# One step of a streaming encoder: stores on another queue, output matmuls in turn, other buffer counts, a split compare

## The chip, the cores and the metric

The kernel runs on one core of a Trainium2 chip. A core has TensorE (matmuls, in the profile PE, its weight loads PEld), VectorE (DVE), ScalarE (ACT), GpSimd (POOL) and SyncE (SP), which only issues DMAs here. The metric is device microseconds of one execution: the median of the runs.

## The reference

One layer with width 1024 for 1,152 rows: 1,024 of a prompt and 128 of 8 decoding requests with 2,048 cached rows each. Everything is fp32.

```
n1 = rmsnorm(h);  z = n1 @ w_in  -> q_a k_a v_a | forget logits | q_b k_b v_b | gate_a gate_b
A: 8 heads x 64, causal, logit += sum of log f between key and query   (keys and queries normalised)
B: 8 heads x 64, own chunk of 64 and the 8 before it, clipped relative bias
m = sigmoid(gate_a)*(y_a @ w_up_a) + sigmoid(gate_b)*(y_b @ w_up_b);   h += m @ w_out
h += PEER(rmsnorm(h))     # per head: top 16 of 128 keys in each of two halves, top 16 of their sums,
                          # softmax g; sum over 8 x 16 of g*gelu(u[idx].x)*v[idx], 16,384 experts
h += sigmoid(rmsnorm(h) @ w_ple_gate) * (p @ w_ple_proj)
```

The outputs are h for both groups of rows, and the new keys, values and log forget values of both branches.

## The kernel before, in words

Rows go in 9 tiles of 128 (tile 8 holds the decoding rows), in two groups: tiles 8, 0, 1, 2, then tiles 3 to 7. The instructions of each engine run in order, and that order is set when the kernel is built, by a scheduler that takes the operations by priority and by its own model of time; `high_priority(offset=...)` with a negative offset marks filling work.

Stages for the first group: norm, attention (`attention_phase`), merge with gates, routing (top 16 of keys on VectorE). Then the second group through the same stages, while under them the experts of the first group's tiles are fetched row by row: GpSimd issues an indirect DMA (L813) into a ring of 4 buffers, VectorE multiplies and accumulates (L816, L818). There are 1,024 of these gathers; 400 are laid as filling before the second attention, the other 624 are tied to steps of the last loop. The second group's experts are computed densely: 36 of 128 hidden blocks (`hidden_phase`) as filling in the second routing, stored to DRAM (L974); then `expand_phase` builds the routing weights as a sum of products of one-hot rows; then `dense_phase` loops over 128 blocks of 128 experts.

Attention runs over 8 units of two heads, four of branch A and four of branch B. `project` makes for each tile of a unit keys, queries and values (three matmuls per slice, split into high and low parts), normalises them (a power on GpSimd, L217), stores the keys and values to the outputs (L328, L329), transposes them, copies the keys into `kT` (L345) and scales the queries into `qp` (L348). In the first group, keys and values of prompt tiles also go to DRAM for the second group (L350, L351). The scores of a tile follow one unit later (`prompt`, or `decode` for tile 8): for each of the two heads scores, minimum, exponential, scaling, transposes (`pt`, L494) copied to `pT` by ScalarE, and the product with the values into one half of the columns of bank `po` (L497). Both heads share `po`, taken at the start of `prompt`. In branch A a second matmul adds the forget sums, with the stationary operand `sel_p`, a constant selector of 8 x 128 columns made at the start by GpSimd (`setup_masks`, L141 called at L169 and L170) and VectorE (L171).

`decode` loads the cache in tiles of 256 KB into buffers with tag `kc` (L522, L586; `KC` = 15 of them, which the temporaries of `setup_masks` use first). Its four requests per pass go to four groups of 32 columns in turn (L547, L591).

In `expand_phase` each of 80 blocks of 8 entries makes one-hot rows `oa` of the first index (L917) and `ob` of the second (L920) on VectorE, scales the first by the routing weight (`ga`, GpSimd L924 and ScalarE L929 in alternate blocks), multiplies on TensorE (L933) and copies to `stage` (L935), stored per half tile (L939).

The DMAs of loads and stores all go through SyncE's queue, in order, except the indirect ones.

Of the kernel before, what the change touches and what calls it, by code (L numbers as in the profile page):

```python
# [18 lines left out]
P = 128  # L19
# [5 lines left out]
GROUPS = ([8, 0, 1, 2], [3, 4, 5, 6, 7])  # L25
DENSE = (3, 4, 5, 6, 7)
PRE = tuple(range(3, 128, 4)) + tuple(range(1, 128, 32))
KC = 15
NP = 4
SM = 6  # L30
PB = (2, 2)
# [15 lines left out]
def build(tc, I, O, dbg=None, stop=None):  # L47
# [44 lines left out]
    nc.vector.memset(m_corner[64:128, :], BIG)  # L92
    m_new = [const.tile([P, P], BF, name=f"m_new{s}") for s in range(2)]
    m_blk = [const.tile([P, P], BF, name=f"m_blk{s}") for s in range(2)]
    sel_p = const.tile([P, 8, P], F32R, name="sel_p")
    qn = const.tile([P, 2], F32, name="qn")
    kn = const.tile([P, 2, P], F32, name="kn")
    bfv = const.tile([P, 8], F32, name="bfv")
# [31 lines left out]
    def setup_masks(dec):  # L130
# [18 lines left out]
        for s in range(2):  # L149
# [10 lines left out]
            nc.vector.tensor_tensor(c, c, d_, op=OP.min)  # L160
            nc.vector.tensor_tensor(a, a, c, op=OP.max)
            nc.vector.tensor_copy(m_new[s], a)
        for q in range(2):
            t1 = tmp(f"t1{q}").rearrange("p (h c) -> p h c", h=4)
            t2 = tmp(f"t2{q}").rearrange("p (h c) -> p h c", h=4)

            o3 = one.rearrange("p (h c) -> p h c", h=4)
            for t, off in ((t1, 4 * q), (t2, 32 + 4 * q)):
                keep(t, o3, [[-1, 4], [0, P]], 0.0, -off, 1)  # L169
                keep(t, t, [[1, 4], [0, P]], 0.0, off, -1)  # L170
            nc.vector.tensor_tensor(sel_p[:, 4 * q:4 * q + 4, :], t1, t2, op=OP.add)  # L171
        for q in range(2):
            t1 = tmp(f"t1{q}s").rearrange("p (h c) -> p h c", h=4)
            t2 = tmp(f"t2{q}s").rearrange("p (h c) -> p h c", h=4)
# [85 lines left out]
    def attention_phase(g, tiles, aT, yT):  # L260
# [17 lines left out]
        def load_unit(u):  # L278
            br = u // 4
            ws = wload(I["wu"][u], 8, 384, f"wu{g}{u}", extra=I["wfl"] if u == UNITS[0] else None,  # L280
                       eng=nc.vector if (u == UNITS[0]) == (g == 0) else None) if g == 0 else wload(I["wu"][u], 8, 384, f"wu{g}{u}", extra=I["wfl"] if u == UNITS[0] else None, eng=nc.gpsimd if u in UNITS[0:NP] else None)
            kT = at.tile([P, WK], F32, tag="kT", name=f"kT{g}{u}")
            vU = at.tile([P, npr + (TS in tiles), P], F32, tag="vU", name=f"vU{g}{u}")
            hi = min(x for x in tiles if x != TS)
            if hi > 0:
                lo = 0 if br == 0 else max(0, hi - 4)
                if lo < hi:
                    nc.sync.dma_start(kT[:, lo * P:hi * P], kT_d[u, :, lo * P:hi * P])
                    nc.sync.dma_start(vU[:, lo:hi, :], v_d[u, :, lo:hi, :])
            Dn = None  # L290
            if br == 1:
                Dn = at.tile([P, 2, 256], F32, tag="Dn", name=f"Dn{g}{u}")
                nc.sync.dma_start(Dn, I["biasP"][u - 4])
                for h in range(2):
                    hh = 2 * (u - 4) + h
                    nc.vector.tensor_scalar(Dn[:, h, :], Dn[:, h, :], rb0[:, hh:hh + 1], -1.0,
                                            op0=OP.subtract, op1=OP.mult)
                    nc.vector.memset(Dn[0:64, h, 192:256], BIG)
            return ws, kT, vU, Dn

        def project(u, n, t, ws, kT, vU, Dn):
# [23 lines left out]
            else:  # L325
                ko = None
            if ko is not None:
                nc.sync.dma_start(ko[rows, cu * P:(cu + 1) * P], kq[:, 0:P])  # L328
                nc.sync.dma_start(vo[rows, cu * P:(cu + 1) * P], vt)  # L329
            tp = bank(f"tp{nm}")  # L330
            nc.tensor.transpose(tp[:, 0:P], kq[:, 0:P], ident)
            nc.tensor.transpose(tp[:, P:2 * P], kq[:, P:2 * P], ident)
            qp = at.tile([P, 2, P], F32, tag="qp", name=f"qp{nm}", bufs=2 * nts if g == 0 else nts + 1)
            nc.gpsimd.memset(qp, 0.0)
            if t == TS:
                kTs = at.tile([P, P], F32, tag="kTs", name=f"kTs{nm}")
                nc.scalar.copy(kTs, tp[:, 0:P])
                q4 = qp.rearrange("p a c -> p (a c)").rearrange("p (b h i) -> p b h i", b=8, h=2)
                for h in range(2):
                    s = slice(64 * h, 64 * h + 64)  # L340
                    nc.scalar.activation(q4[s, :, h, :], tp[s, P:2 * P].rearrange("p (b i) -> p b i", i=16),
                                         AF.Copy, scale=qn[s, br:br + 1])
                pending.append(decode(u, br, qp, kTs, vU[:, slot[TS], :], n, at, dec, yT))
            else:
                nc.scalar.copy(kT[:, t * P:(t + 1) * P], tp[:, 0:P])  # L345
                for h in range(2):
                    s = slice(64 * h, 64 * h + 64)
                    nc.scalar.activation(qp[s, h, :], tp[s, P:2 * P], AF.Copy, scale=qn[s, br:br + 1])  # L348
                if g < len(GROUPS) - 1:
                    nc.sync.dma_start(kT_d[u, :, t * P:(t + 1) * P], kT[:, t * P:(t + 1) * P])  # L350
                    nc.sync.dma_start(v_d[u, :, t, :], vt)  # L351
                pending.append([lambda: prompt(g, u, br, t, n, qp, kT, vU, Dn, at, yT)])

        def order(p):
# [25 lines left out]
    def logf(g, tiles, fl, at, dec):  # L380
# [29 lines left out]
            nc.tensor.transpose(ps[0:40, 0:P], l40[:, i, :], ident)  # L410
            nc.scalar.copy(lT[:, i, :], ps[0:40, 0:P])
        for i, t in enumerate(tiles):
            nc.sync.dma_start(O["lf"][:, t * P:(t + 1) * P], lT[0:8, i, :])
        pt = [t for t in tiles if t != TS]
        if pt:
            i0 = tiles.index(pt[0])
# [35 lines left out]
    def prompt(g, u, br, t, n, qp, kT, vU, Dn, at, yT):  # L452
# [1 line left out]
        nk = t + 1 if br == 0 else min(t, 4) + 1  # L454
        k0 = t + 1 - nk
        W = nk * P
        po = bank(f"po{nm}")
        both = W <= 512 and wide[0] == 1024
        for h in range(2):
            if h == 0 or not both:  # L460
# [2 lines left out]
            for c0 in range(0, W, 512):  # L463
# [2 lines left out]
                rhs = kT[:, k0 * P + c0:k0 * P + c1]  # L466
                if br == 0:
                    nc.tensor.matmul(N[:, c0:c1], qp[:, h, :], rhs, start=True, stop=False)
                    nc.tensor.matmul(N[:, c0:c1], sel_p[:, 2 * u + h, :], cP[:, c0:c1], start=False, stop=not last)
                    if last:  # L470
                        nc.tensor.matmul(N[:, W - P:W], ident_b, m_diag, start=False, stop=True)
                else:
# [17 lines left out]
            for j0 in range(0, nk, 4):  # L490
# [2 lines left out]
                for j in range(j0, j1):  # L493
                    nc.tensor.transpose(ps[:, (j - j0) * P:(j - j0 + 1) * P], p[:, j * P:(j + 1) * P], ident)  # L494
                evac(pT[:, j0:j1, :], ps[:, 0:(j1 - j0) * P].rearrange("p (j c) -> p j c", c=P))
            for j in range(nk):
                nc.tensor.matmul(po[64 * h:64 * h + 64, 0:P], vU[:, k0 + j, 64 * h:64 * h + 64], pT[:, j, :],  # L497
                                 start=j == 0, stop=j == nk - 1)
        nc.scalar.copy(yT[:, u, n * P:(n + 1) * P], po[:, 0:P])

    def decode(u, br, qp, kTs, vU, n, at, dec, yT):
# [383 lines left out]
    def expand_phase():  # L885
# [22 lines left out]
        for n, t in enumerate(DT):  # L908
            rb, gT = ready
            for c0 in range(0, P, W):  # L910
                if c0 % 64 == 0:
# [2 lines left out]
                oa = ex.tile([P, 2, P, 4], BF, tag="oa", name=f"oa{t}_{c0}")  # L914
                ga = ex.tile([P, W, P], F32, tag="ga", name=f"ga{t}_{c0}")
                ob = ex.tile([P, W, P], F32, tag="obb", name=f"obb{t}_{c0}")
                nc.vector.tensor_tensor(oa, iota_i.unsqueeze(1).broadcast_to([P, 2, P, 4]),  # L917
                                        rb[:, 0, cw].rearrange("p (b c) -> p b c", b=2).unsqueeze(2).broadcast_to([P, 2, P, 4]),
                                        op=OP.is_equal)
                nc.vector.tensor_tensor(ob, iota, rb[:, 1, cw].unsqueeze(2).broadcast_to([P, W, P]), op=OP.is_equal)  # L920
                for b in range(2):
                    if (c0 // W) % GD == 0:
# [13 lines left out]
                if c0 == 64 and n + 1 < len(DT):  # L936
                    ready = prepare(DT[n + 1])
                if c0 % 64 == 64 - W:
                    nc.sync.dma_start(G_d[2 * n + c0 // 64], stage)  # L939
        st.close()  # L940

    nsp = -(-TD // 512)
# [26 lines left out]
    def hidden_phase(dn, n2h, n2l):  # L969
        with tc.high_priority(offset=FILL):  # L970
            for q, j in enumerate(PRE):
                ge = dn.tile([P, TD], F32, tag="ge", name=f"gp{j}")
                hidden(dn, ge, j, n2h, n2l, nc.gpsimd, True)
                nc.sync.dma_start(ge_d[q], ge)  # L974

    def dense_phase(hp, yacc, n2h, n2l):

# [219 lines left out]
```

## Time and profile before

| | |
|---|---|
| median of 3 runs | 4042.02 us (4021.49 to 4048.87) |
| the profiled execution | 4036.04 us, span 4033.9 us |
| granted TensorE clock, mean | 0.966 |
| TensorE busy | 3674.5 us (91% of the span) |
| VectorE busy | 2939.1 us (73%) |
| GpSimd busy | 1865.5 us (46%) |
| ScalarE busy | 1446.2 us (36%) |
| DMA | 1002.50 MB, 249 GB/s over the span |

Busy time of an engine is the union of its instructions; matmuls are pipelined, so a single one lasts longer than its distance to the next. A window row gives busy time and count of instructions for a stretch. In rows of waits, "A <- B: total, times, longest" says that A's engine stood idle until B ended. SPq and POOLq are the queues from which DMAs are issued.

### The profile page before, as it was taken

To read this page: it belongs to the slowest core of one execution; us is meant where nothing else is said; L and a number is where in the kernel's file an instruction comes from. 1 tells how busy PE (TensorE), PEld (TensorE's weight loads), DVE (VectorE), ACT (ScalarE), POOL (GpSimd) and SP (SyncE) were. 2 spreads that over 40 slices of the span, in tenths; PEclk is the share of its full clock that TensorE was granted. 3 is DMA by queue.
4 is the path that set the end of the run, shared out by engine and by line. 5 is a ranking of instruction groups with operands and counts; after the bars stand their busy time and mean duration, and the time that the engine had idled before them with its cause. 6 is when DMAs were issued, how large, how long until landed. Compare 5 with 4: busy or idle time off the path is not lost.

```text
span 4033.9 us, 57386 instructions
## 1 busy us (share of the span) xinstructions
PE 3674.5 (91%) x20520; PEld 3032.9 (75%) x20520; DVE 2939.1 (73%) x5531; ACT 1446.2 (36%) x3307; POOL 1865.5 (46%) x1440
## 2 busy tenths in 40 slices
PE   7998899868888798899898899999999999999989
PEld 6555567656676565699898888888888888888866
DVE  5122202899887776889998698888888888888862
ACT  5444422346555510223488422222222222222231
POOL 5111032127667655553276355555555555555510
PEclk9999999879999999899999999999999999999999
DMA  6777733328888888983345789988989898989942
GB/s 207 239 237 208 229 96 120 103 74 262 276 284 263 285 317 297 329 268 115 109 189 219 274 307 310 320 311 310 330 313 317 307 325 314 325 302 307 313 159 72
DMA packets 415118, 1002.50 MB, mean 249 GB/s; under 512 B 38816, under 2 KB 170352, under 8 KB 412400
## 3 DMA queue, kind: packets, MB, share of 16 engines
q0 software_dynamic: 147456, 536.94, 38.7%
q1 hardware_dynamic: 267376, 461.90, 34.4%
q8 instruction: 161, 2.64, 0.3%
q14 instruction: 125, 1.02, 0.1%
HBM read 917.19 MB, written 81.50 MB: 248 GB/s over the span
## 4 chain that ended last, share of the span: by engine, by line
PE 30%; DVE 19%; DMA 19%; issue 18%; POOL 12%; ACT 2%; SPq 0%; POOLq 0%; DVEq 0%; ACTq 0%
DMA v<-in_pv,gi 7%; POOL u L813 6%; DMA u<-in_pu,gi 6%; PE hd L964 5%; POOL v L813 3%; DVE gya L818 3%; DVE u L816 3%; PE pg L933 3%; PE Sd L547 2%; PE py L1015 2%; PE py L1017 2%; PE py L1016 2%; PE pu L638 1%; DMA vs<-in_pv 1%; PE z L209 1%
## 5 line engine op out<-in xcount | busy, mean ns | idle before, releaser
L813 POOL DMA_INDIRECT v<-in_pv,gi x512 | 680.3, 1329 | 582.8 <-DVE gya L818 451.2
L813 POOL DMA_INDIRECT u<-in_pu,gi x512 | 663.4, 1296 | 505.7 <-DVE u L816 374.8
L816 DVE SCALAR_TENSOR_TENSOR u<-u,gn 128x1024 f32<-128x1024 f32 x512 | 628.2, 1236 | 169.0 <-DMA u<-in_pu,gi 167.3
L818 DVE SCALAR_TENSOR_TENSOR gya<-v,hid,gya 128x1024 f32<-128x1024 f32 x512 | 661.3, 1292 | 120.0 <-DMA v<-in_pv,gi 115.5
L1015 PE MATMUL py<-vh,wh 128*128 128x512 f32 x1280 | 507.7, 398 | 44.2 <-ACT wh L946 23.6
L964 PE MATMUL hd<-aTh,uh 128*128 128x320 f32 x2048 | 485.1, 314 | 24.0 <-ACT gp L967 13.7
L1017 PE MATMUL py<-vh,wl 128*128 128x512 f32 x1280 | 498.3, 395 | 5.8 <-DVE wl L947 5.5
L1016 PE MATMUL py<-vl,wh 128*128 128x512 f32 x1280 | 502.8, 394 | 0.0
L964 PE MATMUL hd<-aTh,ul 128*128 128x320 f32 x2048 | 484.1, 314 | 5.5 <-DVE ul L947 4.2
L964 PE MATMUL hd<-aTl,uh 128*128 128x320 f32 x2048 | 484.1, 313 | 0.0
L964 PEld LDWEIGHTS hd<-aTh,uh 128*128 128x128 f32 x2048 | 351.9, 191 | 35.1 <-ACT gp L967 15.0
L964 PEld LDWEIGHTS hd<-aTh,ul 128*128 128x128 f32 x2048 | 349.6, 190 | 12.6 <-DVE ul L947 6.9
L964 PEld LDWEIGHTS hd<-aTl,uh 128*128 128x128 f32 x2048 | 351.3, 191 | 4.0
L1015 PEld LDWEIGHTS py<-vh,wh 128*128 128x128 f32 x1280 | 242.9, 190 | 102.3 <-ACT wh L946 29.7
L946 ACT CAST vh<-vs 128x1024 fp32r<-128x1024 f32 x128 | 134.0, 1052 | 483.3 <-DMA vs<-in_pv 241.9
L1017 PEld LDWEIGHTS py<-vh,wl 128*128 128x128 f32 x1280 | 243.2, 190 | 61.2 <-DVE wl L947 10.6
L1016 PEld LDWEIGHTS py<-vl,wh 128*128 128x128 f32 x1280 | 242.9, 190 | 46.9
L946 ACT CAST uh<-us 128x1024 fp32r<-128x1024 f32 x128 | 134.2, 1048 | 293.0 <-PE hd L964 285.3
L946 ACT CAST wh<-ge 128x640 fp32r<-128x640 f32 x128 | 91.9, 727 | 402.7 <-DVE ge L993 213.4
L1018 DVE TENSOR_TENSOR yacc<-yacc,py 128x1024 f32<-128x1024 f32 x160 | 192.5, 1215 | 15.0 <-PE py L1017 15.0
L497 PE MATMUL po<-pT,vU 128*64 128x128 f32 x1056 | 153.0, 290 | 34.6 <-ACT pT L80 34.0
L933 PE MATMUL pg<-obb,ga 128*128 128x128 f32 x1280 | 158.8, 279 | 26.5 <-POOL ga L924 19.5
(1051 smaller groups left out, 7361.0 us busy)
## 6 DMA issues: line engine op xcount, KB each, us to landing
us<-in_uT SPq DMA_DIRECT2D x128, 512.0 KB
vs<-in_pv SPq DMA_DIRECT2D x128, 512.0 KB
G_d<-stage SPq DMA_DIRECT2D x10, 4096.0 KB
gj<-G_d SPq DMA_DIRECT2D x64, 640.0 KB
kcd<-in_kA SPq DMA_DIRECT2D x128, 256.0 KB
vcd<-in_vA SPq DMA_DIRECT2D x128, 256.0 KB
ge_d<-gp SPq DMA_DIRECT2D x36, 320.0 KB
ge<-ge_d SPq DMA_DIRECT2D x36, 320.0 KB
```

What stands on the lines that cost most here:

```text
L497: nc.tensor.matmul(po[64 * h:64 * h + 64, 0:P], vU[:, k0 + j, 64 * h:64 * h + 64], pT[:, j, :], start=j == 0, stop=j == nk - 1)
L547: nc.tensor.matmul(ps[32 * b4:32 * b4 + 32, :], q3[:, 4 * s + b4, :], rhs, start=br == 1 and q < nch, stop=True)
L813: nc.gpsimd.indirect_dma_start(out=r, out_offset=None, in_=I["pu" if k < P else "pv"], in_offset=bass.IndirectOffsetOnAxis(ap=gi[:, kk:kk ...
L816: nc.vector.scalar_tensor_tensor(r, r, 1.0, n2, op0=OP.mult, op1=OP.mult, accum_out=hid[:, kk:kk + 1])
L818: nc.vector.scalar_tensor_tensor(ya, r, hid[:, kk:kk + 1], ya, op0=OP.mult, op1=OP.add)
L933: nc.tensor.matmul(pg[:, c * P:(c + 1) * P], ga[:, b0 + c, :], ob[:, b0 + c, :], start=True, stop=True)
L946: nc.scalar.copy(out_h, src)
L964: nc.tensor.matmul(ps[sp][:, 0:Nw], a[:, k, :], b[:, k, sp * Nw:(sp + 1) * Nw], start=k == 0 and q == 0, stop=k == 7 and q == 2)
L1015: nc.tensor.matmul(py[:, c], wh[:, ns], vh[:, c], start=a, stop=False)
L1016: nc.tensor.matmul(py[:, c], wh[:, ns], vl[:, c], start=False, stop=False)
L1017: nc.tensor.matmul(py[:, c], wl[:, ns], vh[:, c], start=False, stop=z)
L1018: nc.vector.tensor_tensor(yacc[n], yacc[n], py, op=OP.add)
```

## The change

`KC` goes from 15 to 18. `sel_p` becomes 8 columns wide, built by four selects over 8 columns, and is repeated over 128 columns where it is read. `qp` has 6 buffers in place of 8 in the first group, `Dn` (bias) one in place of two. The stores of keys, values, log forget values, the scratch keys and values, the hidden blocks and the routing weights move from SyncE to ScalarE's queue; that of the keys stands behind the copy to `kT`. In `prompt` the products with the values come after both heads' transposes, the two heads in turn for each block of keys, and `po` is taken there. `oa` is made by two compares of 512 columns in place of one of 1,024.

```diff
-KC = 15
+KC = 18
-    sel_p = const.tile([P, 8, P], F32R, name="sel_p")
+    sel_p = const.tile([P, 8], F32R, name="sel_p")
-        for q in range(2):
-            t1 = tmp(f"t1{q}").rearrange("p (h c) -> p h c", h=4)
-            t2 = tmp(f"t2{q}").rearrange("p (h c) -> p h c", h=4)
-            o3 = one.rearrange("p (h c) -> p h c", h=4)
-            for t, off in ((t1, 4 * q), (t2, 32 + 4 * q)):
-                keep(t, o3, [[-1, 4], [0, P]], 0.0, -off, 1)
-                keep(t, t, [[1, 4], [0, P]], 0.0, off, -1)
-            nc.vector.tensor_tensor(sel_p[:, 4 * q:4 * q + 4, :], t1, t2, op=OP.add)
+        t1 = tmp("t1")[:, 0:8]
+        t2 = tmp("t2")[:, 0:8]
+        for t, off in ((t1, 0), (t2, 32)):
+            keep(t, one[:, 0:8], [[-1, 8]], 0.0, -off, 1)
+            keep(t, t, [[1, 8]], 0.0, off, -1)
+        nc.vector.tensor_tensor(sel_p, t1, t2, op=OP.add)
...
-                Dn = at.tile([P, 2, 256], F32, tag="Dn", name=f"Dn{g}{u}")
+                Dn = at.tile([P, 2, 256], F32, tag="Dn", name=f"Dn{g}{u}", bufs=1)
...
             if ko is not None:
-                nc.sync.dma_start(ko[rows, cu * P:(cu + 1) * P], kq[:, 0:P])
-                nc.sync.dma_start(vo[rows, cu * P:(cu + 1) * P], vt)
+                nc.scalar.dma_start(vo[rows, cu * P:(cu + 1) * P], vt)
...
-            qp = at.tile([P, 2, P], F32, tag="qp", name=f"qp{nm}", bufs=2 * nts if g == 0 else nts + 1)
+            qp = at.tile([P, 2, P], F32, tag="qp", name=f"qp{nm}", bufs=nts + 2 if g == 0 else nts + 1)
...
                 nc.scalar.copy(kT[:, t * P:(t + 1) * P], tp[:, 0:P])
+                if ko is not None:
+                    nc.scalar.dma_start(ko[rows, cu * P:(cu + 1) * P], kq[:, 0:P])
...
-                    nc.sync.dma_start(kT_d[u, :, t * P:(t + 1) * P], kT[:, t * P:(t + 1) * P])
-                    nc.sync.dma_start(v_d[u, :, t, :], vt)
+                    nc.scalar.dma_start(kT_d[u, :, t * P:(t + 1) * P], kT[:, t * P:(t + 1) * P])
+                    nc.scalar.dma_start(v_d[u, :, t, :], vt)
...
-            nc.sync.dma_start(O["lf"][:, t * P:(t + 1) * P], lT[0:8, i, :])
+            nc.scalar.dma_start(O["lf"][:, t * P:(t + 1) * P], lT[0:8, i, :])
...
-        po = bank(f"po{nm}")
+        pTs = []
...
-                    nc.tensor.matmul(N[:, c0:c1], sel_p[:, 2 * u + h, :], cP[:, c0:c1], start=False, stop=not last)
+                    nc.tensor.matmul(N[:, c0:c1], sel_p[:, 2 * u + h:2 * u + h + 1].broadcast_to([P, P]), cP[:, c0:c1], start=False, stop=not last)
...
-            for j in range(nk):
-                nc.tensor.matmul(po[64 * h:64 * h + 64, 0:P], vU[:, k0 + j, 64 * h:64 * h + 64], pT[:, j, :],
-                                 start=j == 0, stop=j == nk - 1)
+            pTs.append(pT)
+        po = bank(f"po{nm}")
+        for j in range(nk):
+            for h, pT in enumerate(pTs):
+                r = slice(64 * h, 64 * h + 64)
+                nc.tensor.matmul(po[r, 0:P], vU[:, k0 + j, r], pT[:, j, :], start=j == 0, stop=j == nk - 1)
...
-                nc.vector.tensor_tensor(oa, iota_i.unsqueeze(1).broadcast_to([P, 2, P, 4]),
-                                        rb[:, 0, cw].rearrange("p (b c) -> p b c", b=2).unsqueeze(2).broadcast_to([P, 2, P, 4]),
-                                        op=OP.is_equal)
+                for b in range(2):
+                    nc.vector.tensor_tensor(oa[:, b, :, :], iota_i,
+                                            rb[:, 0, c0 + 4 * b:c0 + 4 * b + 4].unsqueeze(1).broadcast_to([P, P, 4]), op=OP.is_equal)
...
-                    nc.sync.dma_start(G_d[2 * n + c0 // 64], stage)
+                    nc.scalar.dma_start(G_d[2 * n + c0 // 64], stage)
...
-                nc.sync.dma_start(ge_d[q], ge)
+                nc.scalar.dma_start(ge_d[q], ge)
```

## Rows read from the trace of the kernel before

**Rows 1.** Busy time by stage: stretch, its length, engines with instructions, clock, DMA share, GB/s

```profile
core 0: us, PE busy (x) PEld busy (x) DVE busy (x) ACT busy (x) POOL busy (x), PEclk, DMA share, GB/s
17.00:505.00 488.00, 428.32 (x3379) 285.32 (x3378) 135.74 (x370) 242.33 (x820) 111.46 (x137) 0.96 0.75 223
700.00:890.00 190.00, 139.78 (x599) 113.78 (x598) 171.66 (x939) 76.28 (x202) 31.48 (x32) 0.85 0.27 86
890.00:1395.00 505.00, 443.41 (x2524) 341.93 (x2522) 425.05 (x820) 301.76 (x850) 354.83 (x301) 0.96 0.83 270
1395.00:1690.00 295.00, 254.37 (x933) 176.87 (x934) 219.97 (x312) 47.70 (x65) 160.39 (x134) 0.94 0.88 310
1690.00:2015.00 325.00, 293.36 (x1824) 282.88 (x1822) 302.75 (x1270) 114.65 (x191) 130.31 (x79) 0.93 0.54 178
2015.00:2165.00 150.00, 146.18 (x1163) 145.39 (x1164) 137.52 (x100) 122.75 (x318) 104.45 (x55) 0.99 0.53 202
2257.00:3860.00 1603.00, 1543.96 (x8193) 1367.66 (x8192) 1370.88 (x1513) 376.56 (x535) 850.01 (x621) 0.99 0.90 314
```

**Rows 2.** Waits of TensorE from 17 to 505 us: total, times, longest

```profile
PE pod L591 <- DMA vcd<-in_vA: 25.6, 22, 2.4
PE z L209 <- ACT vU L318: 13.0, 3, 9.2
```

**Rows 3.** Selects at L141 (ns min/median/max, first to last start), then instructions in time

```profile
L141 POOL TENSOR_SCALAR_AFFINE_SELECT t<-one x4: 635/661/705, 25.9 to 28.1; 128x512 f32<-128x512 f32 x4
L141 POOL TENSOR_SCALAR_AFFINE_SELECT t<-t x4: 631/636/677, 34.3 to 38.5; 128x512 f32<-128x512 f32 x4
...
34.92 1.02 POOL L217 TENSOR_TENSOR kq048r<-kq048r,half 128x4 f32<-128x4 f32 x1
36.76 0.69 PE L209 MATMUL z<-wu04h,aTh 128*128 128x392 f32 x1 [9.20 <-ACT vU L318]
```

**Rows 4.** Output matmuls in time (start, us), then busy time of L497 by stage

```profile
1215.63 1.74 PE L497 MATMUL po<-pT,vU 128*64 128x128 f32 x14 [0.35 <-ACT pT L80]
346.74 3.04 PE L591 MATMUL pod<-vcd,pTd 128*32 128x128 f32 x102 [0.16 <-ACT pTd L80]
...
17.00:505.00 488.00, 33.22 (x192) 21.14 (x192) 0.96 0.75 223
890.00:1395.00 505.00, 118.36 (x859) 95.58 (x857) 0.96 0.83 270
```

**Rows 5.** Gathers (L813) by stretch: GpSimd busy (count); then VectorE's use, 890 to 1395

```profile
890.00:1395.00 505.00, 283.80 (x229) 0.96 0.83 270
1395.00:1690.00 295.00, 156.54 (x130) 0.94 0.88 310
1500.00:1600.00 100.00, 56.94 (x49) 0.98 0.87 301
...
L816 DVE SCALAR_TENSOR_TENSOR u<-u,gn 128x1024 f32<-128x1024 f32 x128 | 161.1, 1264 | 31.2 <-DMA u<-in_pu,gi 30.8
```

**Rows 6.** Waits in SyncE's queue over the span: total, times, longest

```profile
SPq L974 <- ACT gp L967: 172.8, 25, 16.9
SPq L329 <- ACT vU L318: 141.8, 36, 16.9
SPq L328 <- DVE kq L316: 90.3, 31, 12.0
```

**Rows 7.** A key store on SyncE's queue: ns min/median/max, first to last start

```profile
L328 SPq DMA_DIRECT2D out_kA<-kq x36: 332/344/1157, 63.7 to 1276.5; - x36
```

**Rows 8.** A round of the one-hot loop in time; a wait for the compare; a 512-wide row

```profile
2209.32 3.48 POOL L924 TENSOR_TENSOR ga<-oa,gT 128x512 f32<-128x512 bf16 x2 [2.24 <-ACT stage L935]
2212.84 0.69 DVE L917 TENSOR_TENSOR oa<-iota_i,rb 128x1024 bf16<-128x1024 bf16 x1 [0.94 <-POOL ga L924]
2214.99 2.08 POOL L924 TENSOR_TENSOR ga<-oa,gT 128x512 f32<-128x512 bf16 x1 [2.19 <-PE pg L933]
...
POOL ga L924 <- DVE oa L917: 11.5, 7, 6.2
...
L789 DVE TENSOR_TENSOR oh<-oh 128x512 bf16<-128x512 bf16 x20 | 12.4, 622 | 0.1
```

More of the change, by code (lines that the diff above doesn't have):

```diff
@@ L345, in project @@
                 nc.scalar.copy(kT[:, t * P:(t + 1) * P], tp[:, 0:P])
+                if ko is not None:
+                    nc.scalar.dma_start(ko[rows, cu * P:(cu + 1) * P], kq[:, 0:P])
                 for h in range(2):
```

## Prediction

> **What bounds the kernel now.** I first cut the span into its stages, by the lines that run in each, and read the busy time of every engine per stage [rows 1]. The reader is to see there that no engine bounds the whole. The first attention (17 to 505) is TensorE's: 428 of 488 us busy, VectorE 136. Routing of the first group (700 to 890) is VectorE's, 172 of 190. The second attention (890 to 1395) has TensorE at 443 of 505, but VectorE at 425 as well. The second merge (1395 to 1690) is TensorE's again; routing of the second group (1690 to 2015) is VectorE's, 303 of 325; the expert loop (2257 to 3860) holds 1544 of 1603 us on TensorE, and no line of the diff runs in it. So the change can only pay in the two attentions, at the start, and in 1690 to 2257.
>
> Second, who TensorE waited for in the first attention [rows 2]: 25.6 us for cached values still on their way, 13.0 us for ScalarE's copy of a value tile, 9.2 of them in one piece at 27 to 37 us [rows 3]. Third, the two kinds of probability-times-value matmuls in order of time [rows 4]. Fourth, how many gathers start in each stage [rows 5], because 400 of the 1,024 gathers are laid as filling under everything from 890 us on. Fifth, what SyncE's queue stood for [rows 6] and what one store costs it [rows 7]. Last, one round of the one-hot loop [rows 8].
>
> **Start: the selector.** Eight selects over 512 columns go (4 x 0.661 + 4 x 0.636 = 5.2 us of GpSimd [rows 3]); four over 8 columns come. No row has 8 columns; between nothing and the old price each, I take a quarter, as start-up must dominate. This matters because GpSimd's queue holds the power for the first row norms: it runs at 34.92 behind four of those selects and one more (3.3 us), and TensorE's stall ends right after, at 36.76 [rows 3]. Gain: 3.3 x 3/4 = 2.5, say **-3 us** (bounds 0 and -5.2). Its use as a stationary operand with a repeated column changes no count of loads; I cost it at nothing.
>
> **Two heads' outputs in turn.** Today 14 such matmuls in a row, all into the same 64 columns of the array, take 1.74 us, 0.124 each; in decode, where four neighbours go to four different quarters of 32 columns, 102 take 3.04 us, 0.030 each [rows 4]. Four quarters together cost what one half costs alone, so instructions on different columns run at the same time. With two halves in turn I expect 0.124 per pair, 0.062 each (bounds: 0.124, no overlap, and 0.062, both at once). There are 1,056 of them: 192 in the first attention and 864 in the second (859 recorded) [rows 4]. TensorE saves 192 x 0.062 = 12 us there and 864 x 0.062 = 54 us here. In the first attention TensorE is the bound, so **-12 us** (bounds 0, -12). The output bank is also taken later, after both heads' transposes, which frees a bank for these; the price is that both transposed tiles live until the end, with only two buffers. I count these against each other.
>
> **Stores on ScalarE's queue, more cache buffers.** 56 key and 56 value stores, 24 + 24 to the scratch tensors and 9 of gates leave SyncE; 92 of these 169 fall in the first attention, 77 in the second. What SyncE loses on them is not the issue, 0.34 us each [rows 7], but standing: 141.8 us for the value copy and 90.3 for the keys [rows 6], with the next loads queued behind. Without them, and with 18 cache buffers in place of 15 (a score pass loads 16 tiles), loads start earlier; the smaller query and bias buffers that pay for them give back some depth. The stake is the 25.6 us of [rows 2]; I take half, **-13 us** (bounds 0, -25.6). The Trainium skill speaks against this: its page "DMA: Bandwidth & Descriptors", section "Issuing engines are not separate DMA queues", says that all queues end on the same 16 DMA engines and that issuing from several saves only the issuing sequencer's time, usually small. By that rule this term would be nothing. The rows show something the rule leaves out, the in-order wait before the issue, so I keep half.
>
> ScalarE pays. No row shows a store on its queue; SyncE's 0.344 us is the nearest [rows 7]. In the first attention 92 x 0.344 = 32 us come on top of 242 busy of 488 [rows 1]. They stand behind copies that TensorE needs (value tile, key tile), and what follows them, the query scaling, is used one unit later; that is the cover. If it were gone all 32 us would count. I take **+4 us** (bounds 0, +32). Each store waits for data already made: the value or key copy just ahead of it on the same engine, or keys that the transposes have already read. Queued behind it are the query copies and the next softmax.
>
> **The second attention.** TensorE needs 54 us less, but the gathers don't. The stage starts 229 gathers in 505 us, 0.453 per us; the merge after it, where VectorE has far less else to do, 130 in 295, 0.441; the best 100 us have 49 [rows 5]. So the gathers already go at about their own pace, and VectorE works them off in order between the softmax steps. If the order of instructions keeps 229 of them in the stage, it can shrink to 229 / 0.49 = 467 us at best, -38, and not at all at the merge's pace. If they are pushed out instead, 54 x 0.453 = 24 gathers of 1.26 us on VectorE [rows 5] = 31 us land in the routing stage, whose VectorE has 22 us free of 325 [rows 1]: net 54 - 31 = -23. Between 0, -23 and -38 I take **-16 us**. The 77 stores (26 us on ScalarE, 302 of 505 busy) hide behind the gathers' pace; without that cover they are the slower rival below.
>
> **Routing to expansion.** SyncE's 172.8 us of standing for the hidden activations [rows 6] go, but TensorE is busy 293 of 325 and 146 of 150 there [rows 1]. The one-hot compare becomes two of 512. Nearest row: 512 bf16 at 0.622 us [rows 8], so 1.24 against 0.69; lower bound, no cost. In a late round the compare is done at 2213.5 and GpSimd needs it only at 2214.99, after TensorE [rows 8]: 1.46 us of cover. In 2015 to 2165 VectorE has 12.5 us free and ran 100 instructions [rows 1], two a block, so 50 of the 80 blocks: 50 x 0.55 = 27.5, so up to +15; against it, GpSimd's 11.5 us of waiting for this compare could go [rows 8]. I take **0**.
>
> **Sum**: -3 - 12 - 13 + 4 - 16 = **-40 us**. The profiled execution took 4036.04 us (span 4033.9), so 3996; it lies 6 us below the median 4042.02, so on the median's scale 4002. I predict **4000 us**, own range 3980 to 4020.
>
> **Rivals.**
> *All of it arrives*: cached values never late and gathers at their best pace: -3 - 12 - 25.6 + 4 - 38 = -75, 3961 us. For it: 49 gathers in 100 us do occur. Against: no whole stage holds that pace.
> *ScalarE becomes the bound (slower)*: the stores stand in its in-order queue ahead of the softmax of both attentions. All 169 x 0.344 = 58 us on the path and no gain in the second attention: -3 - 12 - 13 + 58 = +30, 4066 us; with a quarter of SyncE's 232 us of standing [rows 6] moved along, 4124. It decides from 44 / 169 = 0.26 us per store on the path, where the gains are used up. Against: ScalarE is busy half and 60% of the two stages.
> *Loads gain nothing* (the shared-engines rule as a mechanism here: transfers, not the queue, are late): 4000 + 13 = 4013 us. The DMA engines are 75% busy in that stage [rows 1], which fits either.
> *The halves don't overlap*: no 12 and no 16: 4028 us. Against: the decode matmuls [rows 4].
> *Nothing moves the end*: 4042 us; the attention would have to be bound by VectorE or loads throughout.
>
> **Chances.** Forecast 0.42, all arrives 0.15, loads gain nothing 0.12, no overlap 0.07, nothing 0.05, ScalarE 0.19. A measurement of this kernel tells about 1%, 40 us, from no change: below 4002 lie all of the second and two thirds of the forecast's cases, 0.43; above 4082 some three quarters of ScalarE's, 0.15; between, 0.42. Range 3945 to 4065: it leaves out the worst of ScalarE's cases and little below.
>
> **What would show it.** Pairs of output matmuls at about 0.06 us each; the first attention ending 20 to 30 us earlier, with waits for cached values about half; the second attention shorter by 10 to 25 us at an unchanged 0.45 to 0.47 gathers per us; the stall at 27 to 37 us shorter by about 3; the expert loop at 1603 us. It is wrong if ScalarE's stores cost well over 0.34 us or TensorE waits for ScalarE much more; if the gathers pile up in the routing stage; or if the new order of instructions changes the expert loop.

## The result, and the profile after

The changed kernel takes 4000.59 us in the median of 10 runs (3988.24 to 4012.65), the kernel before 4037.78 beside it (10 runs, 4021.49 to 4048.87): ratio 0.9917, interval 0.9901 to 0.9932, so 0.8% faster. The predicted time of 4000 is met; by the bound of 1% named there the outcome is "no change". The profiled execution after took 3997.34 us (span 3995.6, mean granted clock 0.962).

To see where 38 us of span went, both traces are cut at the same marks of the program instead of at the same times: the last decode output (end of the first attention), the first gather, the last output matmul (end of the second attention), the last merge matmul, the last top index, the first matmul of the expansion, the expert loop. The columns are those of [rows 1]. First the kernel before, then the changed one:

```profile
17.00:503.00 486.00, 427.41 (x3373) 284.87 (x3375) 135.74 (x370) 240.71 (x817) 111.21 (x136) 0.96 0.75 223
892.70:1391.50 498.80, 440.58 (x2517) 340.80 (x2516) 419.53 (x799) 297.89 (x842) 351.94 (x299) 0.96 0.83 271
1391.50:1685.50 294.00, 253.91 (x930) 176.06 (x929) 218.74 (x309) 47.63 (x64) 159.99 (x134) 0.94 0.88 309
1685.50:2023.80 338.30, 302.20 (x1872) 291.40 (x1871) 313.08 (x1281) 121.51 (x208) 139.04 (x85) 0.93 0.54 181
2279.70:3874.00 1594.30, 1537.05 (x8111) 1358.61 (x8112) 1368.93 (x1510) 370.62 (x527) 849.39 (x621) 0.99 0.90 312
```

```profile
17.00:467.40 450.40, 405.08 (x3377) 279.44 (x3375) 131.47 (x369) 238.92 (x817) 107.49 (x134) 0.96 0.80 240
859.20:1335.70 476.50, 400.80 (x2526) 305.42 (x2525) 406.91 (x796) 295.62 (x846) 330.19 (x286) 0.94 0.82 270
1335.70:1622.30 286.60, 253.53 (x934) 175.45 (x930) 217.78 (x290) 47.99 (x65) 158.92 (x131) 0.93 0.89 313
1622.30:1980.40 358.10, 316.88 (x1973) 305.27 (x1972) 339.60 (x1313) 123.76 (x210) 166.83 (x102) 0.94 0.59 199
2237.10:3834.80 1597.70, 1537.02 (x8111) 1360.30 (x8112) 1368.93 (x1510) 370.93 (x527) 847.50 (x621) 0.99 0.89 311
```

The first attention is 35.6 us shorter with the same matmuls: TensorE is busy 22.3 us less and idle 13.3 us less (58.6 to 45.3). The second attention is 22.3 us shorter, though TensorE's work in it fell by 39.8. The merge gains 7.4. Routing of the second group then gives 19.8 back, the expert loop, in which no line changed, 3.4, and the stretches that the rows leave out 3.8. That 3.4 means little: over the traces with all their gathers laid as before, the loop takes 1584 to 1605 us.

In the first attention, TensorE's costliest groups; before first, and only the two that matter, since the third stands in [rows 4]:

```profile
L547 PE MATMUL Sd<-kcd,qp 128*32 128x512 f32 x320 | 100.5, 615 | 1.8 <-DVE Nd L557 1.2 <-DMA kcd<-in_kA 0.6
L591 PE MATMUL pod<-vcd,pTd 128*32 128x128 f32 x1280 | 52.0, 284 | 26.9 <-DMA vcd<-in_vA 25.6 <-ACT pTd L80 1.1
```

```profile
L550 PE MATMUL Sd<-kcd,qp 128*32 128x512 f32 x320 | 89.7, 603 | 0.7 <-DMA kcd<-in_kA 0.7
L594 PE MATMUL pod<-vcd,pTd 128*32 128x128 f32 x1280 | 43.0, 274 | 5.0 <-DMA vcd<-in_vA 3.1 <-ACT pTd L80 1.8
L501 PE MATMUL po<-pT,vU 128*64 128x128 f32 x192 | 28.3, 325 | 16.7 <-ACT pT L80 16.6
```

The wait for cached values is almost gone (25.6 to 3.1, [rows 2]). What the prediction had not looked at is the busy time: decode's score matmuls (`Sd`) cost 10.8 us less and its output matmuls (`pod`) 9.0 less, with the same counts. The prompt's output matmuls (`po`) give 4.9, and 9 us more are waited for ScalarE's copies in front of them; decode's transposes (`ptd`, L579) take 6.3 back (27.1 to 33.4). How the same `Sd` matmuls can cost different times is seen in the kernel before, in order of time (start, length):

```profile
201.60 1.07 PE L547 MATMUL Sd<-kcd,qp 128*32 128x512 f32 x8
...
211.03 1.06 PE L547 MATMUL Sd<-kcd,qp 128*32 128x512 f32 x6
212.02 0.33 PE L494 MATMUL pt<-ident,p 128*128 128x128 f32 x1
212.27 1.05 PE L547 MATMUL Sd<-kcd,qp 128*32 128x512 f32 x2
```

One matmul of a request leaves two records, so x8 is all four requests, each on its own 32 columns of the array: 1.07 us together. At 211.03 three run (x6) and the fourth follows alone behind another matmul (x2): 1.06 + 1.05, twice the cost. TensorE waits for nothing there. Its order is fixed when the kernel is built, so it is the scheduler that put the other matmul between them; that it did so because its model has the fourth tile come late is an inference, and that the tile was late in the run is not shown. The price is paid as busy time and not as idle time, since a lone quarter costs as much as four. Over the stage the kernel before has 91 such bursts (records of `Sd` that start one after the other), 53 of them with one or two records; the changed one 87 and 46. Bursts of all four are not more but fewer (13 and 9): what goes is short ones.

The other lines that answer to the prediction's are of the changed kernel too, but for one: the output matmuls of one head, six records, of the kernel before.

```profile
104.40 0.87 PE L497 MATMUL po<-pT,vU 128*64 128x128 f32 x6
```

The changed kernel in order of time, the start and some output matmuls of both attentions:

```profile
25.31 0.49 POOL L141 TENSOR_SCALAR_AFFINE_SELECT t<-one 128x8 f32<-128x8 f32 x2
32.28 0.35 POOL L141 TENSOR_SCALAR_AFFINE_SELECT t<-t 128x8 f32<-128x8 f32 x2
33.51 1.02 POOL L215 TENSOR_TENSOR kq048r<-kq048r,half 128x4 f32<-128x4 f32 x1
35.35 0.69 PE L207 MATMUL z<-wu04h,aTh 128*128 128x392 f32 x1 [8.03 <-ACT vU L316]
...
104.54 0.43 PE L501 MATMUL po<-pT,vU 128*64 128x128 f32 x2
105.49 0.87 PE L501 MATMUL po<-pT,vU 128*64 128x128 f32 x10
...
155.95 0.43 PE L501 MATMUL po<-pT,vU 128*64 128x128 f32 x2 [3.69 <-ACT pT L80]
157.34 1.54 PE L501 MATMUL po<-pT,vU 128*64 128x128 f32 x10
...
1202.98 1.09 PE L501 MATMUL po<-pT,vU 128*64 128x128 f32 x14
```

The power runs at 33.51 and the stall ends at 35.35, 1.4 us earlier than in [rows 3]. 14 output matmuls take 1.09 us where they took 1.74 [rows 4]. The ten at 157.34 take 1.54 us where the same ten at 105.49 take 0.87; TensorE has just waited 3.69 us for ScalarE, and the granted clock is 0.50, the lower of its two levels (1.2 GHz):

```profile
157.30:158.70 1.40, 1.40 (x11) 1.14 (x10) 0.00 (x0) 0.58 (x1) 0.00 (x0) 0.50 0.97 256
```

By stretch, TensorE's time on L501 around the second attention, then GpSimd's on the gathers (L816) in the second attention, the merge, and routing up to the last top index:

```profile
850.00:1400.00 550.00, 61.57 (x864) 49.26 (x864) 0.93 0.82 271
...
859.20:1335.70 476.50, 261.18 (x214) 0.94 0.82 270
1335.70:1622.30 286.60, 156.74 (x128) 0.93 0.89 313
1622.30:1847.40 225.10, 79.66 (x63) 0.95 0.76 255
```

L501's 61.57 us stand against 119.81 in the same stretch before; the gathers, 214, 128 and 63, against 227, 131 and 48. TensorE's whole work in the second attention fell by less than L501's, 39.8 against 58.2, for the other matmuls cost more there (the 96 of L468 655 ns in the mean, 628 before) at a granted clock of 0.94 where it was 0.96. Last, a value store on ScalarE's queue (ns min/median/max), the answer to [rows 7]:

```profile
L326 ACTq DMA_DIRECT2D out_vA<-vU x36: 338/339/397, 63.6 to 1225.8; - x36
```

### The profile page after: what moved, and what is told of

The parts are those of the page before. It is cut to its first block, busy times and chain, and to the rows that moved or that the text cites. A ratio compares the mean times of both kernels' runs of the same rounds, so it can differ in the third digit from the quotient of the medians.

```text
span 3995.6 us, 57332 instructions
## 1 busy us (share of the span) xinstructions
PE 3616.7 (91%) x20520; PEld 2993.2 (75%) x20520; DVE 2956.2 (74%) x5610; ACT 1438.8 (36%) x3307; POOL 1848.0 (46%) x1436
## 4 chain that ended last, share of the span: by engine, by line
DVE 23%; issue 21%; DMA 21%; PE 20%; POOL 13%; ACT 2%; POOLq 0%; ACTq 0%; SPq 0%; DVEq 0%
DMA v<-in_pv,gi 9%; POOL u L816 7%; DMA u<-in_pu,gi 6%; POOL v L816 4%; DVE gya L821 4%; DVE u L819 4%; PE pg L936 2%; PE Sd L550 2%; DMA vs<-in_pv 1%; PE pu L641 1%; PE hd L967 1%; POOL ga L927 1%; PE z L207 1%; DVE topi L735 1%; PE z L209 1%
## 5 line engine op out<-in xcount | busy, mean ns | idle before, releaser
L816 POOL DMA_INDIRECT v<-in_pv,gi x512 | 668.6, 1306 | 597.6 <-DVE gya L821 442.5
L816 POOL DMA_INDIRECT u<-in_pu,gi x512 | 673.9, 1316 | 500.5 <-DVE u L819 359.4
L1018 PE MATMUL py<-vh,wh 128*128 128x512 f32 x1280 | 510.3, 400 | 60.8 <-DVE yacc L1021 39.8
L967 PE MATMUL hd<-aTh,uh 128*128 128x320 f32 x2048 | 485.0, 314 | 13.9 <-ACT gp L970 12.2
L936 PEld LDWEIGHTS pg<-obb,ga 128*128 128x128 f32 x1280 | 152.2, 191 | 42.8 <-POOL ga L927 20.7
```

The lines of the kernel that those rows point to most:

```text
L816: nc.gpsimd.indirect_dma_start(out=r, out_offset=None, in_=I["pu" if k < P else "pv"], in_offset=bass.IndirectOffsetOnAxis(ap=gi[:, kk:kk ...
L936: nc.tensor.matmul(pg[:, c * P:(c + 1) * P], ga[:, b0 + c, :], ob[:, b0 + c, :], start=True, stop=True)
L967: nc.tensor.matmul(ps[sp][:, 0:Nw], a[:, k, :], b[:, k, sp * Nw:(sp + 1) * Nw], start=k == 0 and q == 0, stop=k == 7 and q == 2)
L1018: nc.tensor.matmul(py[:, c], wh[:, ns], vh[:, c], start=a, stop=False)
```

## The experiments

Two theories stood at first: the gain is the stores' leaving SyncE's queue together with the pairs, as predicted; or it is the number of cache buffers. (Letters in the expectations hold for their own run.) The change was split into its four separable parts; one by one on the kernel before, they make up the whole diff. "Attention 1" is the length from 17 us to the last decode output. It is read, like the other stages, from one execution of each kernel, while the times are medians.

**Pairs alone.** The diff's lines in `prompt` from `pTs = []` to the loop over heads, nothing else.

> The kernel before with one part of the change alone: the two heads' products with the values in turn. My account (the second attention runs at the gathers' own pace): output matmuls at about 0.06 us each; the last decode output 10 to 12 us earlier; the second attention shorter by some 20 us, and most of that given back in the routing behind it; in all -15 to -25 us, ratio 0.994 to 0.996. Rival (TensorE bounds both attentions, its saving of 60 us arrives): -35 us or more, ratio 0.991 or less.

4048.73 us, ratio 1.0026 (1.0011 to 1.0042). The pairs do overlap (L501 at 63.09 us from 850 to 1400, 119.81 before), the second attention falls from 498.8 to 467.8 us, and routing grows from 338.3 to 368.5, by the same 30. Attention 1 is 10 us longer: its score matmuls fall into 99 bursts, 63 of them short, and cost 105.8 us (100.5 before), and 8.5 us are waited for ScalarE's scaled probabilities ahead of the transposes (1.3 before). Why the order came out so was not found. The end is neither what was expected (-15 to -25 us) nor the rival's. GpSimd's gathers of this run, in the second attention and in routing up to the last top index:

```profile
907.60:1375.40 467.80, 259.41 (x209) 0.94 0.83 269
...
1663.90:1899.10 235.20, 83.41 (x68) 0.94 0.76 257
```

That is 18 gathers fewer and 20 more than before, at nearly the same pace (209 / 467.8 = 0.447 per us, 0.455 before).

**Stores alone.** Every `nc.sync.dma_start` of a store that the diff moves becomes `nc.scalar.dma_start`.

> The kernel before with the stores on ScalarE's queue alone. My account (SyncE's standing held back the cache loads): waits of TensorE for cached values, 25.6 us in the first attention, fall to about 12, the last decode output 8 to 13 us earlier, the second attention unchanged, total -8 to -12 us. Rival one (all queues end on the same DMA engines, only issue time is saved): 0, waits unchanged. Rival two (ScalarE pays): 0 to +30 us, with waits for ScalarE up.

4041.18 us, 1.0008 (0.9990 to 1.0026). Attention 1 is unchanged (486.1), though the wait for cached values does fall:

```profile
PE pod L593 <- DMA vcd<-in_vA: 16.8, 18, 1.8
PE z L209 <- ACT vU L318: 14.4, 4, 10.6
PE po L499 <- ACT pT L80: 12.4, 7, 2.9
```

The three rows are TensorE's waits from 17 to 505 us [rows 2]: 8.8 us less for values, but 4.8 more for ScalarE's copies ahead of the output matmuls (7.6 before), 1.4 more at the start, and SyncE's loads then stand for buffers instead: 47.4 us on the output matmuls where it was 24.3. The end is as rival one had it, though the waits are not unchanged.

**Buffers alone.** `KC = 18`, with the narrow selector, `qp` and `Dn` that make room for it.

> The kernel before with the buffer counts alone (18 cache buffers, narrow selector, fewer query and bias buffers). My account: the stall of TensorE near 27 to 37 us shorter by 3 us, waits for cached values fall by a third to a half even with the stores left on SyncE, last decode output 5 to 12 us earlier, total -5 to -12. Rival (the queue's standing and not the buffers bounds the loads): -3 us from the selector alone.

3998.43 us, 0.9910 (0.9889 to 0.9930): all of the gain, and three times or more what was expected of it (-5 to -12). Attention 1 is 453.8 us, 32.2 shorter. The second attention is some 13 us shorter as well, with the output matmuls unpaired and a granted clock of 0.98; what does that is not shown.

**Two compares alone.** The `oa` lines.

> The kernel before with the two compares alone. My account: nothing in time, -2 to +3 us, the one-hot loop of the same length within 3 us. Rival one (VectorE is loaded near full there): +10 to +15 us. Rival two (the new order of instructions moves other stages by itself): stages far from the edit move by 5 us or more.

4035.42 us, 1.0003 (0.9986 to 1.0020).

The buffer part still holds four edits. **The narrow selector alone** (`sel_p` lines, `KC` 15), and **all of the buffer part but the size** (`KC` stays 15):

> The kernel before with the narrow selector alone, 15 cache buffers. If the third of a start-up stall is all it gives: -2 to -4 us, the last decode output 2 to 4 us earlier. Rival (the freed GpSimd time and cache buffers at the start put the whole first attention in another order): -10 us or more, or the other way.

> The buffer part of the change but for the cache buffers, which stay 15: narrow selector, six query buffers, one bias buffer. If the 18 cache buffers carry the gain of the buffer part (32 us at the last decode output): -2 to -5 us here, as with the selector alone, or slower because the query buffers are fewer. Rival (a looser start or the query buffers carry it, by another order of instructions): -20 us or more already here.

4047.62 us, 1.0030 (1.0013 to 1.0048), and 4041.61 us, 1.0020 (1.0004 to 1.0035). So one number, 15 to 18, is worth 43 us (4041.61 to 3998.43). The two kernels, attention 1, `KC` 15 and then 18, in executions of 4059.2 and 3988.61 us, farther apart than their medians; last, SyncE's wait for a buffer for the next cached keys, in the same order:

```profile
L545 PE MATMUL Sd<-kcd,qp 128*32 128x512 f32 x320 | 102.9, 617 | 2.1 <-DMA kcd<-in_kA 2.1
L589 PE MATMUL pod<-vcd,pTd 128*32 128x128 f32 x1248 | 50.7, 283 | 25.0 <-DMA vcd<-in_vA 23.7 <-ACT pTd L80 1.1
```

```profile
L545 PE MATMUL Sd<-kcd,qp 128*32 128x512 f32 x320 | 84.5, 625 | 2.2 <-DMA kcd<-in_kA 2.2
L589 PE MATMUL pod<-vcd,pTd 128*32 128x128 f32 x1280 | 49.1, 282 | 16.5 <-DMA vcd<-in_vA 15.3 <-ACT pTd L80 1.2
...
SPq L520 <- PE Sd L545: 45.1, 41, 5.0
SPq L520 <- PE Sd L545: 21.0, 24, 2.5
```

18.4 us of busy score matmuls and 8.4 of waiting for values, in an attention 1 of 490.6 and 453.8 us. The key loads stand half as long for buffers that `Sd` has yet to free: 45 us against 21 here, 49 in the kernel before against 22 in the changed one. One thing these runs do not separate: with another `KC` the scheduler also lays TensorE's instructions in another order, so what the buffers give while the kernel runs and what the new order gives is not told apart. The two compares alone, an edit far behind, leave attention 1 in the order of the kernel before (91 bursts, 53 short), and it ends 3 us earlier: so much a stage differs from one execution to the next.

The narrow selector saves 0.8 us at the start (TensorE's stall ends at 35.96) and is still a little slower; its weight load in the score matmuls takes 190 ns in both forms, and TensorE is granted a lower clock in its attention 1 (0.94 against 0.96 before). What sets that stays open.

**The changed kernel with 15 buffers**, the test from the other side:

```diff
-KC = 18
+KC = 15
```

> The changed kernel with 15 cache buffers in place of 18; everything else of the change stays. Theory A (the gain of the change is the three further cache buffers, which let the tiles of all four requests be there together in the first attention): the whole gain goes, 4035 to 4048 us, ratio 1.000 to 1.003; the score matmuls of the first attention cost about 100 us of TensorE again (100.5 before, 89.7 with the change) and the first attention ends near 503 us. Rival B (the gain is the edits together, the paired outputs and ScalarE's stores need each other and the buffers only help): about half stays, 4015 to 4025 us.

4026.20 us, 0.9979 (0.9960 to 0.9997). Attention 1 is back at 488.1 us with 100.8 us of score matmuls and 20.9 of waiting for values:

```profile
L550 PE MATMUL Sd<-kcd,qp 128*32 128x512 f32 x320 | 100.8, 618 | 2.2 <-DMA kcd<-in_kA 2.2
```

The first attention is as theory A had it, the end lies between the two theories, nearer to B. Most of the gain goes (0.9917 to 0.9979, some 25 of 37 us), but not all: 9.9 us are left, by the interval 1 to 16. Whether the pairs and the stores gave them is not shown: in the profiled execution the expert loop, in which no line differs, is 9 us shorter than before (1585 against 1594), while the second attention and routing nearly cancel (-17 and +16). With 18 buffers the other parts leave nothing (0.9910 without, 0.9917 with).

**Order or number?** If a lone quarter is what costs, the loads could also be ordered: the same quarter of all four requests one after the other, where today all quarters of one request come first. Once on the changed kernel, once on the kernel before.

```diff
-for b4 in range(4):
-    for q in range(4):
-        (load request b4's quarter q)
+for q in range(4):
+    for b4 in range(4):
+        (load request b4's quarter q)
```

> The changed kernel with 18 cache buffers, its first-group key loads issued quarter by quarter (the same quarter of all four requests one after the other) in place of request by request; the transfers and the matmuls are the same. Theory A (four score matmuls run together only where the four requests' tiles of one quarter are there together, so the order of arrival is what costs): the score matmuls fall from 89.7 us of TensorE to 50 to 75, the first attention ends 10 to 25 us earlier than 467, of which the routing stage gives back up to half; 3980 to 3995 us, ratio 0.986 to 0.990. Rival B (the buffers' number alone matters, since the loads are ahead far enough with 18): within 3 us of the changed kernel, 4000 us, ratio 0.992.

> The kernel before, 15 cache buffers, with the first-group key loads issued quarter by quarter. Theory A (order of arrival): the last tile of a pass is late for one quarter only and not for one request's four quarters, so three quarters' matmuls run together; score matmuls 60 to 85 us against 100.5, first attention 20 to 35 us earlier than 503, 4005 to 4020 us, ratio 0.992 to 0.996. Rival B (a pass needs 16 tiles and has 15 buffers, and the wait for the last is what costs, in whatever order they come): 4030 to 4040 us, ratio 0.998 to 1.001.

With 15 buffers 4031.80 us, 0.9995 (0.9981 to 1.0009), score matmuls at 103.6 us in 109 bursts: the order of the loads alone does nothing, as rival B had it. With 18, 3996.51 us, 0.9905 (0.9889 to 0.9922), no different from the changed kernel, though the matmuls do close up: 75 bursts in place of 87, and 23 of all four in place of 9. Its attention 1, the score matmuls' group, and the longest of TensorE's waits:

```profile
17.00:473.00 456.00, 395.75 (x3377) 279.98 (x3376) 131.26 (x369) 237.18 (x817) 107.71 (x134) 0.94 0.83 237
```

```profile
L550 PE MATMUL Sd<-kcd,qp 128*32 128x512 f32 x320 | 77.3, 624 | 2.2 <-DMA kcd<-in_kA 1.3 <-ACT p L447 0.8
```

```profile
PE po L501 <- ACT pT L80: 25.2, 9, 6.1
```

TensorE is busy 9.3 us less than in the changed kernel and idle 14.9 more (60.3 against 45.3), 8.6 of them for ScalarE's copies ahead of the output matmuls. So lone quarters explain busy time, but in this pair of kernels less busy time did not bring the end of the stage forward. What sets it at 18 buffers is not settled. The rate of the stage, 220 to 225 GB/s in every kernel with 15 buffers and 237 to 240 in every kernel with 18, does not settle it either: the bytes are the same, so the rate only tells the length over again.

**The gathers.** Why do 22 us of the second attention not reach the end? The gathers of two of the four first-group tiles are left out (their expert output is missing) and none are laid ahead of the expert loop, on the kernel before and on the changed one:

> The kernel before with the gathers of two of the first group's four tiles left out (their expert sum is missing in the output) and none of the others ahead of the expert loop, so that no gather runs under the second attention, merge and routing. If the gathers set the pace there: the second attention falls from 499 us to about 420 to 450 (TensorE 441 busy there, overlapped), routing ends earlier by the 48 gathers' 60 us. If they don't: 490 us or more for the attention.

> The changed kernel with the same gathers left out (the expert sum of two tiles is missing). If the gathers swallow what the paired matmuls save: the second attention is now shorter than in the kernel before without them by 40 to 55 us, the routing stage is as long in both, and the whole kernel differs by 70 to 90 us. Rival (the saving is lost inside the attention itself, by waits for ScalarE and the two transposed buffers): the attention differs by 15 to 25 us, as with gathers, the whole by 50 to 60.

3896.40 us (0.9663) and 3801.33 us (0.9430): 95 us apart where the full kernels are 37 apart, a little above the 70 to 90 expected if the gathers swallow the saving. From the first score of the first group's routing to the end of the second attention, before and changed:

```profile
756.20:1354.10 597.90, 529.79 (x2932) 415.29 (x2933) 308.17 (x1362) 349.27 (x1006) 88.77 (x100) 0.94 0.14 42
```

```profile
715.90:1266.10 550.20, 478.51 (x2931) 372.07 (x2933) 307.43 (x1362) 341.87 (x1006) 90.43 (x100) 0.94 0.16 46
```

TensorE's 51.3 us of saved matmuls come out as 47.7 us of time, where with gathers 23.2 do (643.2 to 620.0). Routing is 268.1 and 271.3 us: nothing is given back. The saving isn't lost in waits of the attention itself either: TensorE's idle time over this stretch is 68.1 and 71.7 us, while in the second attention with gathers it goes from 58.2 to 75.7. Without the gathers GpSimd's issues, VectorE's sums and the transfers all go at once; which of the three sets the pace is not told apart. The expert loop is 22 us shorter in the second kernel as well (1589.6 and 1567.7), which no line explains; it is a good part of the 95.

**Fewer gathers ahead.** The changed kernel with ordered loads and

```diff
-G0 = 400
-G1 = 5
+G0 = 376
+G1 = 6
```

> As the changed kernel with quarter-by-quarter loads, with 24 filling gathers fewer ahead of the expert loop (376 in place of 400), which the expert loop takes in its place (six to a step in place of five at most). Theory A (the routing stage gives back what the attentions save, since the gathers that no longer fit beside the shorter attentions run there, on VectorE): the routing stage falls from 358 to 335 to 345 us, and if the expert loop hides the 24, the end comes 10 to 22 us earlier than with quarter-by-quarter loads alone, 3965 to 3980 us. Rival B (the expert loop has no more cover for gathers than it uses, or the gathers then end after it): the loop grows by what routing saves, the end within 5 us of quarter-by-quarter loads alone.

4014.25 us, 0.9943 (0.9922 to 0.9965): slower by 18. Routing does shrink, from 356.2 to 315.6 us with 36 gathers in place of 60, 1.7 us for each that is gone. But the loop (2215.2 to 3822.7, gathers first, then all engines) and what follows it:

```profile
2215.20:3822.70 1607.50, 862.23 (x633) 0.99 0.90 312
3822.70:4018.00 195.30, 16.93 (x12) 0.88 0.34 117
...
2215.20:3822.70 1607.50, 1535.69 (x8111) 1358.39 (x8112) 1379.21 (x1526) 371.41 (x528) 863.75 (x634) 0.99 0.90 312
```

It takes 633 gathers in 1607.5 us where it took 620 in 1584.4, and twelve end after it, with the final stage behind them: the last starts at 3854.4, 32 us after the loop's last matmul. In this form the loop has no room for the 24; both theories' times were too low.

## Why the prediction was right, and where not

**The total** was right (3996 forecast for the profiled execution, 3997.34 measured), but that it came within 2 us is luck: the terms were mis-sized in directions that cancel. The first attention gave 35.6 us where -3 - 12 - 13 + 4 = -24 was forecast; the second attention, merge and routing gave 9.9 in place of 16; and 7.2 were lost in stretches that stood at nothing. The mechanism of the second attention held; that of the largest gain, in the first, was mostly another than the one forecast.

**Start, -3**: 1.4 us. The narrow selects cost 0.2 us each (0.84 for four), a third of the old price and not a quarter, and five other selects, of 128 columns, now stand ahead of the power in GpSimd's queue, 0.35 us each.

**Output matmuls, -12 in the first attention**: 4.9. The step that failed is "0.062 each". Runs are short there: twelve records, six for each head, go from two times 0.87 us to 0.43 + 0.87, because the order leaves one block alone at the head of the pair (x2, then x10). It does so in all eight of these; and in four of them the ten run at the lower clock behind a wait of 3.3 to 4.6 us for ScalarE's copy, 1.54 us in place of 0.87. In the second attention the measured 0.071 each (61.57 / 864) is near the forecast, 58 us of these matmuls against 54; TensorE's whole work there fell by 39.8. The page "TensorEngine Tiling (Array Packing)" of the Trainium skill, section "Key Properties", says that different tiles of the array run in parallel; the trace agrees where the matmuls stand next to each other (14 in 1.09 us in turn, 1.74 on one half).

**Loads, -13**: this is the term that failed, in cause and in size. The prediction put it down mainly to SyncE's standing ahead of the loads; taken alone that takes 8.8 us off the wait for values, and nothing off the time (1.0008). The rival "Loads gain nothing" was right for the stores. The Trainium skill's page "DMA: Bandwidth & Descriptors", section "Issuing engines are not separate DMA queues", says that issuing from several engines saves only the issuing time; the end agrees (1.0008), the wait for values does not quite (25.6 to 16.8). But the buffers, named in the same term, gave 32 us in attention 1 alone. The stake was read from idle time only, 25.6 us of [rows 2], when the score matmuls, in bursts that break up, carry another 10.8 of busy time and the cached output matmuls 9.0 (why these is not shown).

**ScalarE, +4**: a store takes 0.339 us on its queue, the forecast's 0.344. TensorE waits 9.0 us more for ScalarE's copies ahead of the output matmuls (7.6 to 16.6), but this is not the stores' price alone: with the stores alone it is 12.4, with buffers alone 8.4, with all but the buffers 6.9, and with the narrow selector alone, where no store moved, 12.2. What the term was worth can't be separated; it lies well under the 32 of its upper bound.

**Second attention, -16**: net. It went as the "pushed out" branch has it: 22.3 us shorter there, 13 gathers fewer in the stage and 15 more in routing, 19.8 given back. That is -2.5 where the branch itself said -23 and the term -16; with 7.4 from the merge, not forecast, the three stages come to -9.9. The pace of gathers stayed at 0.449 per us (214 / 476.5), as forecast, and the runs without them, where 47.7 of 51.3 us come through, show that they hold the stage.

**Routing to expansion, 0**: the first matmul to the last of the expansion takes 232.7 and 233.5 us. The two compares take 0.416 each, 0.83 a round against 1.24 taken.

The rivals: ScalarE as the bound did not come; the pairs do overlap; "all of it arrives" came only for the cached values (3.1 us left); against it stand 9 us more of waiting for ScalarE's copies and the 19.8 of routing.

## What to carry to other kernels

Where matmuls share the array by columns, too few buffers for their operands can show as busy time of TensorE and not only as a wait: look for bursts that break up. Here a pass reads 16 tiles, and 18 buffers in place of 15 gave 0.6 to 1.1%; 16 and 17 were not measured, so whether one full set is the bound is open. Moving stores to another queue gave nothing here: with 15 buffers the loads stood for buffers instead, and with 18 the kernel without that move, and without the pairs, was no slower. And a stage that hides filling work can hardly shrink faster than that work: what was cut from TensorE came back in the next stage with the pushed-out gathers (31 us and 30 with the pairs alone, 22.3 and 19.8 with the whole change).

## What the runs showed of the hardware

A 32-column, 512-wide score matmul costs 1.05 us alone and four on different columns 1.07 us together. Output matmuls on 64 columns: 14 in 1.74 us in a row, 14 in 1.09 with the halves in turn. A store's issue costs 0.339 us on ScalarE's queue and 0.344 on SyncE's. A select over 8 columns takes about 0.2 us, over 512 columns 0.64 to 0.66 [rows 3].
